# Hybrid DeltaNet, window-attention and PEER block on one core: four token blocks gathered instead of three, part of the gathering placed between mixers and retrievals

## The chip, the cores and the metric

The kernel runs on one core of a Trainium2 chip. The time is device microseconds of one execution. Three runs of the kernel before took 3164.12, 3176.35 and 3185.84 us; the median is 3176.35 us. All matrix products are split in two float parts each (a high part and a rest), so one product is three matmuls.

## The reference, cut to what matters

One decoder layer over 1024 tokens of width 1024, in 8 blocks of 128 tokens.

```python
h = rmsnorm(x);  z = h @ W_in                       # projection
o_A = gated_deltanet(...); o_B = sliding_window(...) # the two mixers
x = x + concat(o_A, o_B) @ W_out
# PEER: 16384 single-neuron experts, 8 heads, the best 16 each: 128 experts per token
qry = ht @ wq;  sc = qry . sub_keys;  top_k twice -> expert (T, 8, 16), gates = softmax
act = gelu(einsum("td,thkd->thk", xb, u_tab[eb]))
y   = einsum("thk,thkd->td", gb * act, v_tab[eb])
x = x + y
x = x + sigmoid(rmsnorm(x) @ W_g) * (p @ W_p);  out = rmsnorm(x)
```

Each token needs 128 rows of `u_tab` and 128 rows of `v_tab`. The kernel can get `y` of a block in two ways. **Gathered**: for each of the 128 expert slots, one indirect DMA fetches a row of 4 KB for each of the 128 tokens, and VectorE forms the dot product (u) or adds the weighted row (v). **Dense**: TensorE multiplies the block with all 16384 experts, 128 at a time, and the activations are multiplied with a gate matrix that is zero for all experts not chosen.

## The kernel before, in words

The work is written in program order with a tile framework, which reorders the instructions of each engine by a simulated time line, earlier program text first; on the chip each engine then runs its own list strictly in order. DMAs are issued by SP, the indirect ones by GpSimd (POOL).

- `upstream` (L317): `project` for tokens 0 to 511, the first mixers, `project` for tokens 512 to 1023, then four groups of two blocks: `mixers(gi + 1)` and `retrieve(gi)`. `mixers` calls `deltanet` and `swa` for each block. The projection frees its memory before the first retrieval.
- `retrieve`: the output projection and x, the norm, the queries, the scores, `first_topk` per head and half, then `topk` for each block (L739), which gives the 128 chosen experts and their gates.
- `topk` ends in two ways. For a gathered block (`ABLK`, blocks 5, 6, 7) it writes the experts' numbers into `eidx`. For a dense block (`BBLK`, blocks 0 to 4) it builds the gate matrix on chip: for every 4 tokens two one-hot comparisons on VectorE (`o`), four scalings on ScalarE, four matmuls (`bk_gm`) and a copy into `stage`; a `stage` tile holds `TB` = 32 tokens and is written to `gd` in HBM.
- `dense` (L857) runs over 32 groups of 4 expert tiles. A group loads its gates into `Gt` (one buffer, L879). For each expert tile `ur` and `vr` are loaded (512 KB each) and split (`uh`, `ul`, `vh`, `vl`), 2 x 24 matmuls of 320 columns make `bk_u`, ScalarE applies gelu, VectorE multiplies with `Gt` and makes `wh`, `wl`. After four tiles come the matmuls of 512 columns into `bk_yp` (two blocks, kept in PSUM to the end) and `bk_y` (the other blocks, added into `xB` each time).
- `gather_job` is a Python generator; each step is one indirect DMA `rows` and one VectorE operation (L839 for u, `acc` for v). `dense` takes 6 steps of it after each of its 128 expert tiles, 768 in all. `rows` has 4 buffers in the pool `gp` and, from the second gathered block on, 4 more in `gx`.
- `final` (L925): the gate of the layer input and the last norm, block by block.

Of the kernel before, what the change touches and what calls it, by code (L numbers as in the profile page):

```python
# [7 lines left out]
F32 = mybir.dt.float32  # L8
# [10 lines left out]
P = 128  # L19
T = 1024  # L20
NBLK = 8
D = 1024
DK = 8
NE = 128
# [1 line left out]
NEG = -3.0e38  # L26

GROUPS = [[0, 1], [2, 3], [4, 5], [6, 7]]
ABLK = [5, 6, 7]
BBLK = [0, 1, 2, 3, 4]  # L30
NA = len(ABLK)
GC = 4
TB = 32
GBUF = 4
GXBUF = 4
HELD = 2

CONSTS = ["ident", "ui", "sl", "ones", "iota", "mp"] + ["bm0"]
# [24 lines left out]
def block_kernel(ctx: ExitStack, tc, I, out, dbg=None):  # L63
# [8 lines left out]
    def tt(o, a, b, op):  # L72
        return V.tensor_tensor(o, a, b, op)  # L73
# [253 lines left out]
    def upstream():  # L327
        with early as em:
            dn = em.enter_context(tc.tile_pool(name="dn", bufs=1, reuse_waits="tile"))
            psum(em, dn=2, de=1, sw=1)  # L330
            with ExitStack() as es:
                c1 = es.enter_context(tc.tile_pool(name="c1", bufs=1, side="right"))
                wp = es.enter_context(tc.tile_pool(name="wp", bufs=3, side="right"))
                sm = es.enter_context(tc.tile_pool(name="sm", bufs=2, side="right"))
                psum(es, acc=2, tp=2)
                projected(wp, sm)
                load_consts()
                mixw = row(c1, "mix_norm", D)
                convw = c1.tile([P, 12, 4], F32, name="convw")
                nc.sync.dma_start(convw, I["convw"])  # L340
                onorm = row(c1, "out_norm", P)
                V.tensor_scalar(onorm, onorm, 0.5, None, op0=ALU.mult)
                dtb = row(c1, "dt_bias", 4)
                nea = row(c1, "a_log", 4)
                S.activation(nea, nea, AF.Exp)
                V.tensor_scalar(nea, nea, -1.0, None, op0=ALU.mult)
                prevs = c1.tile([P, 12, 3], F32, name="prevs")
                halo[:] = [(mixw, convw, onorm, dtb, nea), prevs]
                rope_tables(sm, cos, sin)
                project(0, (c1, wp, sm))  # L350
                mixers = mixing(dn)
                mixers(0)
                project(1, (c1, wp, sm))
            with ExitStack() as es:
                lt = es.enter_context(tc.tile_pool(name="lt", bufs=1, side="right", reuse_waits="tile"))
                retrieve = retrieving(lt, es)
                for gi in range(len(GROUPS)):
                    if gi + 1 < len(GROUPS):
                        mixers(gi + 1)
                    retrieve(gi)  # L360
# [20 lines left out]
    def retrieving(lt, es):  # L381
# [14 lines left out]
        def retrieve(gi):  # L396
# [9 lines left out]
            for ti in range(4):  # L406
                cs = slice(ti * 256, (ti + 1) * 256)
                pcs = [bank("s3", [256]) for _ in range(nb)]
                for dh in range(4):
                    wh, wl = weights([w[ti * 2 + dh // 2][:, 2 * (dh % 2):2 * (dh % 2) + 2] for w in woc],  # L410
                                     [P, 2, 256])
                    for bi in range(nb):
                        bs_ = slice(bi * P, (bi + 1) * P)
                        for k in range(2):
                            dk = 2 * dh + k
                            mm3(pcs[bi], mTh[:, dk, bs_], mTl[:, dk, bs_], wh[:, k], wl[:, k],
                                dk == 0, dk == DK - 1)
                for bi in range(nb):
                    tt(xts[bi][:, cs], pcs[bi], xts[bi][:, cs], ALU.add)
            h2 = hp.tile([P, 2, DK, N], F32R, tag="h2", name="h2")  # L420
            h2h, h2l = h2[:, 0], h2[:, 1]
            for bi, b in enumerate(grp):
# [13 lines left out]
            for q4 in range(4):  # L436
                qT = []
                keysT = sm.tile([P, 4, P], F32, tag="keysT", name="keysT", bufs=1)
                nc.sync.dma_start(keysT, I["keysT"][:, 4 * q4:4 * q4 + 4])
                for q in range(4 * q4, 4 * q4 + 4):  # L440
                    whs = [weights([w[q][:, 4 * dh:4 * dh + 4] for w in wqc], [P, 4, P]) for dh in range(2)]
                    pq = bank("s3", [N])
                    for dk in range(DK):
                        wh, wl = whs[dk // 4]
                        mm3(pq, wh[:, dk % 4], wl[:, dk % 4], h2h[:, dk], h2l[:, dk], dk == 0, dk == DK - 1)
                    qt = sm.tile([P, N], F32, tag="qt", name="qt", bufs=4)
                    copy(qt, pq)
                    qT.append(qt)
                for bi in range(nb):
                    pk = bank("s3", [4, P])  # L450
                    for i in range(4):
                        mm(pk[:, i], qT[i][:, bi * P:(bi + 1) * P], keysT[:, i])
                    sc = lt.tile([P, 4, P], F32, tag="sc", name="sc", bufs=2)
                    copy(sc, pk)
                    for i in range(4):
                        first_topk(lt, sc[:, i], tv[bi][:, 4 * q4 + i], tiu[bi][:, 4 * q4 + i])
            for bi, b in enumerate(grp):
                topk(lt, bg, b, tv[bi], tiu[bi])

        return retrieve  # L460

# [51 lines left out]
    def deltanet(dn, dn_state, b, qkv_d, zc_d, g, beta, eg, mTh, mTl, cols):  # L513
        def t4(tag, bufs=1):
            return dn.tile([P, 4, P], F32, tag=tag, name=tag, bufs=bufs)

        qkv = dn.tile([P, 12, P], F32, tag="qkv", name="qkv", bufs=2)
        nc.sync.dma_start(qkv, qkv_d)
        zs = t4("zs")
        nc.sync.dma_start(zs.rearrange("p a b -> p (a b)"), zc_d[:, 0:512])  # L520
# [65 lines left out]
        for l in range(1, 7):  # L586
# [20 lines left out]
            if l < 6:  # L607
                px = bank("dn", [4, P])
                for h in range(4):
                    tr(px[:, h], Y[:, h])  # L610
                X = t4("X")
                copy(X, px)
        kb = scaled("kb", 4, cf[:, 2])
        vb = scaled("vb", 8, cf[:, 3])
        qg = scaled("qg", 0, cf[:, 0])
# [37 lines left out]
    def swa(dn, state, b, zc_d, cos, sin, sink, mTh, mTl, cols):  # L653
# [70 lines left out]
        copy(mTh[:, 4:8, cols], po)  # L724
        tt(mTl[:, 4:8, cols], po, mTh[:, 4:8, cols], ALU.subtract)
        state["kv"] = (kz, vz)

    MP = C["mp"]

# [8 lines left out]
    def topk(tk, bg, b, v, iu):  # L738
# [13 lines left out]
        for h in range(8):  # L752
            c = cand[:, h]
            V.max(out=bs[:, h, 0:8], in_=c)
            V.max_index(out=pu[:, h, 0:8], in_max=bs[:, h, 0:8], in_values=c)
            V.match_replace(out=c, in_to_replace=bs[:, h, 0:8], in_values=c, imm_value=NEG)
            V.max(out=bs[:, h, 8:16], in_=c)
            V.max_index(out=pu[:, h, 8:16], in_max=bs[:, h, 8:16], in_values=c)
        pos = tk.tile([P, 16, 8], BF, tag="pos", name="pos")
        V.tensor_copy(pos.rearrange("p k h -> p h k"), pu)  # L760
        dx = tk.tile([P, 16, 8], BF, tag="dx", name="dx")
# [11 lines left out]
        for k0 in range(0, 16, KC):  # L773
# [11 lines left out]
            tt(ge, bc(st, 1, 16), bc(sel_b[:, 2], 2, KC), ALU.is_equal)  # L785
            tt(t3, ge, bc(ix[:, 1], 2, KC), ALU.mult)
            summed(i2.rearrange("p (h k) -> p k h", h=8)[:, ks], t3)

        ga = gate_a[:, ABLK.index(b)] if b in ABLK else bg.tile([P, P], F32, tag="ga", name="ga")
        gv = ga.rearrange("p (h k) -> p h k", k=16)  # L790
# [16 lines left out]
        for tb in range(P // TB):  # L807
            stage = bg.tile([P, NE, TB], F32, tag="stage", name="stage", bufs=2)
            for t8 in range(TB // NTK):
# [7 lines left out]
                for q in range(NTK // 4):  # L817
# [2 lines left out]
                        mm(pg[:, i], o2[:, 4 * q + i], o1[:, 4 * q + i])  # L820
                    t0 = t8 * NTK + 4 * q
                    copy(stage[:, :, t0:t0 + 4].rearrange("p e t -> p t e"), pg)
            nc.sync.dma_start(gd[(b - BBLK[0]) * (P // TB) + tb], stage)

    def gather_block(gp, a):
# [3 lines left out]
        dots = gp.tile([P, P], F32, tag="dots", name="dots", bufs=1)  # L829

        def rows(tab, s):
            r = (gx if a and s % 2 else gp).tile([P, D], F32, tag="rows", name="rows")
            G.indirect_dma_start(out=r, out_offset=None, in_=tab,  # L833
                                 in_offset=bass.IndirectOffsetOnAxis(ap=eidx[:, a, s:s + 1], axis=0))
            return r
# [14 lines left out]
            yield  # L850
        nc.sync.dma_start(x1d[b], acc)

    def gather_job(gp):
        for a in range(NA):
            yield from gather_block(gp, a)

    def dense(xB):  # L857
        with ExitStack() as es:
            gp = es.enter_context(tc.tile_pool(name="gp", bufs=GBUF, reuse_waits="tile"))
            pp = es.enter_context(tc.tile_pool(name="pp", bufs=1, reuse_waits="tile"))  # L860
            up = es.enter_context(tc.tile_pool(name="up", bufs=2, reuse_waits="tile"))
            ap = es.enter_context(tc.tile_pool(name="ap", bufs=2, reuse_waits="tile"))
# [9 lines left out]
            nparts = (NT + 511) // 512  # L872
            step = (NT // nparts + TB - 1) // TB * TB
            parts = [(n0, min(step, NT - n0)) for n0 in range(0, NT, step)]
            total = NA * 2 * P
            job = gather_job(gp)
            done = 0
            for cg in range(NE // GC):
                Gt = ap.tile([P, NT // TB, GC, TB], F32, tag="Gt", name="Gt", bufs=1)  # L879
                nc.sync.dma_start(Gt.rearrange("p t g k -> p t (g k)"),  # L880
                                  gd[:, :, cg * GC:(cg + 1) * GC, :].rearrange("t p g k -> p t (g k)"))
                vs, ws = [], []
                for ci in range(GC):
# [23 lines left out]
                        copy(wh[:, n0:n0 + n], ge)  # L907
                        tt(wl[:, n0:n0 + n], ge, wh[:, n0:n0 + n], ALU.subtract)
                    ws.append((wh, wl))
                    want = total * (c + 1) // NE  # L910
                    while done < want and next(job, "end") != "end":
                        done += 1
                for bi in range(NB):
                    for j in range(2):
                        cs = slice(j * 512, (j + 1) * 512)
# [6 lines left out]
                                ci == 0 and (cg == 0 or not keep), ci == GC - 1 and (cg == NE // GC - 1 or not keep))  # L922
                        if not keep or cg == NE // GC - 1:
                            tt(xB[:, bi, cs], py, xB[:, bi, cs], ALU.add)
            for _ in job:  # L925
                pass

    def final(xB):
# [52 lines left out]
                post(*cur)  # L981

    upstream()
    gx = ctx.enter_context(tc.tile_pool(name="gx", bufs=GXBUF, side="right", reuse_waits="tile"))
    with tc.tile_pool(name="xB", bufs=1, side="right", reuse_waits="tile") as xp:
        xB = xp.tile([P, NB, D], F32, name="xB")
        dense(xB)
# [60 lines left out]
```

## Time and profile before

| | |
|---|---|
| median of three runs | 3176.35 us (3164.12 to 3185.84) |
| span of the profiled execution, the only time that the profile gives for it | 3163.2 us |
| busy in that span | PE 2984.4, VectorE (DVE) 2601.3, ScalarE (ACT) 1296.5, GpSimd (POOL) 1028.0 us |
| moved by DMA | 869.38 MB, 275 GB/s on average |
| issued in `dense` | 768 gathers (402.70 MB), 128 `ur` and 128 `vr` (512 KB each), 32 `Gt` (1280 KB each) |

PE is TensorE's matmuls, PEld its weight loads. Busy times are unions: an instruction can begin some 0.1 us before the one ahead of it has ended. The DMA share is the mean busy share of the core's 16 DMA engines. The granted clock is a share of 2.4 GHz.

### The profile page before, as it was taken

Reading aid. Unit: us, or ns where it says so; the run is one execution under the profiler, and the core shown is the slowest. Engines: PE = TensorE matmul, PEld = TensorE weight load, DVE = VectorE, ACT = ScalarE, POOL = GpSimd, SP = SyncE. Lnnn points to the kernel's source line nnn. Section 1 sums busy time; section 2 is a strip of 40 time slices with the busy share of each in tenths; the row PEclk is TensorE's granted clock in tenths of the full one; section 3 lists DMA queues with packets and bytes.
Section 4 is the critical chain, followed back from the end, with each engine's and each line's share of the span. In section 5 each row is a group of like instructions: output and inputs, shape, how many; then the busy total and the mean of one; then the engine's idle time right before and its main releaser. Section 6 shows DMA issues by size and latency. Waiting matters only on the chain. (4 is left out here: it accounts for less than half of the span.)

```text
span 3163.2 us, 50802 instructions
## 1 busy us (share of the span) xinstructions
PE 2984.4 (94%) x18287; PEld 2704.4 (85%) x18287; DVE 2601.3 (82%) x6191; ACT 1296.5 (41%) x2761; POOL 1028.0 (32%) x804
## 2 busy tenths in 40 slices
PE   7989989999897889899999999999999999999998
PEld 5878989899897878778888887988899889898887
DVE  6668636999899899789888887988988878799876
ACT  5577534488887862123222222222222122222232
POOL 0000000000000014445455565555565645566600
PEclk9999999999999999999999999999999999999999
DMA  7569566667578678778889888998998888999932
GB/s 232 159 240 353 171 213 225 207 228 248 199 242 321 235 274 283 279 263 298 292 297 316 305 310 310 338 353 304 340 334 309 315 317 321 327 328 345 334 140 87
DMA packets 366188, 869.38 MB, mean 275 GB/s; under 512 B 29296, under 2 KB 153584, under 8 KB 363120
## 3 DMA queue, kind: packets, MB, share of 16 engines
q1 hardware_dynamic: 255344, 463.43, 43.1%
q0 software_dynamic: 110592, 402.70, 35.3%
q8 instruction: 144, 2.36, 0.3%
q14 instruction: 108, 0.88, 0.1%
HBM read 766.40 MB, written 99.61 MB: 274 GB/s over the span
## 5 line engine op out<-in xcount | busy, mean ns | idle before, releaser
L128 PE MATMUL bk_u<-hT,uh 128*128 128x320 f32 x4096 | 919.4, 311 | 16.1 <-ACT ge L904 16.1
L833 POOL DMA_INDIRECT rows<-in_u_dram,eidx x384 | 495.1, 1289 | 893.6 <-DVE tiu L732 469.1
L128 PEld LDWEIGHTS bk_u<-hT,uh 128*128 128x128 f32 x4096 | 698.2, 189 | 36.6 <-ACT ge L904 19.3
L833 POOL DMA_INDIRECT rows<-in_v_dram,eidx x384 | 523.5, 1363 | 401.9 <-DVE acc L76 283.5
L128 PE MATMUL bk_u<-hT,ul 128*128 128x320 f32 x2048 | 635.8, 311 | 0.2 <-DVE ul L73 0.2
L76 DVE SCALAR_TENSOR_TENSOR acc<-rows,dots,acc 128x1024 f32<-128x1024 f32 x384 | 492.0, 1281 | 44.5 <-DMA rows<-in_v_dram,eidx 41.3
L839 DVE CUSTOM_DVE_ANT_0 rows<-rows,h2n 128x1024 f32<-128x1024 f32 x384 | 461.8, 1221 | 37.3 <-DMA rows<-in_u_dram,eidx 31.5
L128 PEld LDWEIGHTS bk_u<-hT,ul 128*128 128x128 f32 x2048 | 387.5, 189 | 5.0 <-DVE ul L73 0.5
L904 ACT ACTIVATE ge<-bk_u 128x320 f32<-128x320 f32 x256 | 110.3, 432 | 642.1 <-PE bk_u L128 541.9
L128 PE MATMUL bk_y<-vh,wh 128*128 128x512 f32 x768 | 313.1, 408 | 40.2 <-DVE xB L73 38.2
L70 ACT ACTIVATE wh<-ge 128x320 fp32r<-128x320 f32 x256 | 119.0, 470 | 525.6 <-DVE ge L73 466.7
L128 PE MATMUL bk_y<-vl,wh 128*128 128x512 f32 x768 | 308.5, 402 | 0.0
L128 PE MATMUL bk_y<-vh,wl 128*128 128x512 f32 x768 | 304.3, 402 | 2.2 <-DVE wl L73 1.8
L128 PE MATMUL bk_gm<-o,o 128*128 128x128 f32 x1280 | 205.4, 292 | 29.6 <-ACT o L70 27.6
L70 ACT ACTIVATE o<-o,tT 128x128 f32<-128x128 f32 x640 | 202.4, 396 | 40.0 <-DVE o L73 34.7
L73 DVE TENSOR_TENSOR o<-iota,tT 128x512 f32<-128x512 f32 x320 | 205.4, 686 | 13.8 <-PE bk_gm L128 12.9
L128 PE MATMUL bk_yp<-vh,wh 128*128 128x512 f32 x512 | 202.3, 400 | 13.5 <-ACT wh L70 13.5
L128 PEld LDWEIGHTS bk_gm<-o,o 128*128 128x128 f32 x1280 | 182.2, 200 | 37.1 <-ACT o L70 33.9
L73 DVE TENSOR_TENSOR ge<-ge,Gt 128x320 f32<-128x320 f32 x256 | 123.7, 487 | 108.7 <-DMA Gt<-gd 95.2
L128 PEld LDWEIGHTS bk_y<-vh,wh 128*128 128x128 f32 x768 | 147.8, 192 | 76.2 <-DVE xB L73 43.2
L128 PE MATMUL bk_s<-h,whi 128*128 128x256 f32 x1024 | 206.8, 294 | 5.2 <-ACT h L70 1.5
L128 PE MATMUL bk_yp<-vl,wh 128*128 128x512 f32 x512 | 201.8, 398 | 0.0
(308 smaller groups left out, 6001.8 us busy)
## 6 DMA issues: line engine op xcount, KB each, us to landing
ur<-in_uT_dram SPq DMA_DIRECT2D x128, 512.0 KB
vr<-in_v_dram SPq DMA_DIRECT2D x128, 512.0 KB
gd<-stage SPq DMA_DIRECT2D x20, 2048.0 KB
Gt<-gd SPq DMA_DIRECT2D x32, 1280.0 KB
wlo<-wqc SPq DMA_DIRECT2D x128, 256.0 KB
whi<-wqc SPq DMA_DIRECT2D x128, 256.0 KB
whi<-woc SPq DMA_DIRECT2D x64, 256.0 KB
wlo<-woc SPq DMA_DIRECT2D x64, 256.0 KB
```

Source lines behind the costliest of these rows:

```text
L70: return S.activation(o, i, AF.Copy, **k)
L73: return V.tensor_tensor(o, a, b, op)
L76: return V.scalar_tensor_tensor(o, a, s, b, op0, op1, **k)
L128: PE.matmul(o, l, r, start=start, stop=stop)
L833: G.indirect_dma_start(out=r, out_offset=None, in_=tab, in_offset=bass.IndirectOffsetOnAxis(ap=eidx[:, a, s:s + 1], axis=0))
L839: V.tensor_tensor_reduce(out=u, in0=u, in1=h2n, op0=ALU.mult, op1=ALU.add, scale=1.0, scalar=0.0, accum_out=dots[:, s:s + 1])
L904: S.activation(ge, pa, AF.Gelu_apprx_tanh)
```

## The change

Blocks 0 to 3 are gathered and blocks 4 to 7 are dense, so there are 1024 gather steps instead of 768, and `dense` works on 512 tokens instead of 640, as one part of 512 columns instead of two of 320. The pool `gp` is opened when the projections are done. `tick(us)` stands at places in the mixers and in the retrieval; it adds `us` x `RATE` (0.55) to a credit, and for each whole credit one gather step is written there, as far as the blocks that are through `topk` allow. What is left is spread over the 128 expert tiles of `dense`. `gx` has 6 buffers, is open from the start of `dense` and serves every second step there. `TB` is 16, and `Gt` has two buffers. `qkv`, the input of `deltanet`, has one buffer instead of two.

```diff
-ABLK = [5, 6, 7]
-BBLK = [0, 1, 2, 3, 4]
+ABLK = [0, 1, 2, 3]
+BBLK = [4, 5, 6, 7]
-TB = 32
+TB = 16
-GXBUF = 4
+GXBUF = 6
+RATE = 0.55
...
                 project(1, (c1, wp, sm))
+            pools["gp"] = ctx.enter_context(tc.tile_pool(name="gp", bufs=GBUF, side="right", reuse_waits="tile"))
...
                     tt(xts[bi][:, cs], pcs[bi], xts[bi][:, cs], ALU.add)
+                    tick(0.5)
...
                         first_topk(lt, sc[:, i], tv[bi][:, 4 * q4 + i], tiu[bi][:, 4 * q4 + i])
+                        tick(1.7)
             for bi, b in enumerate(grp):
                 topk(lt, bg, b, tv[bi], tiu[bi])
+                ready[0] = sum(1 for a in ABLK if a <= b)
+                tick(2.0)
...
-        qkv = dn.tile([P, 12, P], F32, tag="qkv", name="qkv", bufs=2)
+        qkv = dn.tile([P, 12, P], F32, tag="qkv", name="qkv", bufs=1)
...   deltanet, after each of its 6 levels
+            tick(1.0)
...   end of swa
+        tick(6.0)
...   topk: after each of 8 heads, after each of 4 chunks, after each 4 tokens of gates
+            tick(1.2)
+            tick(5.0)
+                tick(1.4)
...
-            r = (gx if a and s % 2 else gp).tile([P, D], F32, tag="rows", name="rows")
+            r = (pools["gx"] if "gx" in pools and s % 2 else gp).tile([P, D], F32, tag="rows", name="rows")
...
+    pools = {}
+    ready = [0]
+    paced = {"credit": 0.0, "done": 0, "job": None}
...
+    def advance(n):
+        if paced["job"] is None:
+            paced["job"] = gather_job()
+        limit = ready[0] * 2 * P
+        while n > 0 and paced["done"] < limit and next(paced["job"], "end") != "end":
+            paced["done"] += 1
+            n -= 1
+
+    def tick(us):
+        paced["credit"] += us * RATE
+        n = int(paced["credit"])
+        paced["credit"] -= n
+        advance(n)
...
-            total = NA * 2 * P
-            job = gather_job(gp)
-            done = 0
+            first = paced["done"]
+            total = NA * 2 * P - first
             for cg in range(NE // GC):
-                Gt = ap.tile([P, NT // TB, GC, TB], F32, tag="Gt", name="Gt", bufs=1)
+                Gt = ap.tile([P, NT // TB, GC, TB], F32, tag="Gt", name="Gt", bufs=2)
...
-                    want = total * (c + 1) // NE
-                    while done < want and next(job, "end") != "end":
-                        done += 1
+                    advance(first + total * (c + 1) // NE - paced["done"])
...
-            for _ in job:
+            for _ in paced["job"]:
                 pass
```

## Rows read from the trace of the kernel before

**Rows 1.** Stages: us, busy PE, PEld, DVE, ACT, POOL (instructions), clock, DMA share, GB/s.

```profile
0.00:625.00 625.00, 578.63 (x4065) 525.35 (x4066) 420.75 (x1357) 340.16 (x828) 8.29 (x32) 0.98 0.68 226
625.00:1161.00 536.00, 481.66 (x3841) 464.55 (x3839) 505.01 (x2104) 439.15 (x1088) 1.03 (x4) 0.96 0.70 244
1161.00:3052.00 1891.00, 1826.91 (x9939) 1635.51 (x9940) 1596.11 (x2496) 476.22 (x778) 1018.64 (x768) 0.98 0.88 310
3052.00:3163.00 111.00, 97.22 (x448) 78.99 (x446) 79.46 (x239) 40.99 (x68) 0.00 (x0) 0.95 0.26 91
```

**Rows 2.** The same view, four short windows.

```profile
700.00:800.00 100.00, 99.13 (x845) 96.98 (x845) 98.73 (x420) 86.58 (x220) 0.00 (x0) 1.00 0.70 240
1000.00:1030.00 30.00, 23.07 (x146) 21.32 (x147) 25.20 (x71) 25.80 (x62) 0.00 (x0) 0.94 0.97 393
1150.00:1180.00 30.00, 18.92 (x106) 18.04 (x107) 26.15 (x111) 12.13 (x19) 8.91 (x7) 0.77 0.87 321
2200.00:2300.00 100.00, 100.00 (x558) 90.27 (x558) 90.00 (x100) 25.03 (x44) 58.25 (x45) 1.00 0.97 345
```

**Rows 3.** The tile `get` of `topk`: ns min/median/max, first to last start.

```profile
L73 DVE TENSOR_TENSOR get<-pos,sel_b x32: 405/418/428, 588.8 to 1620.0; 128x512 bf16<-128x512 bf16 x32
```

**Rows 4.** Groups of instructions: busy us, mean ns | idle before.

```profile
L128 PE MATMUL bk_gm<-o,o 128*128 128x128 f32 x1280 | 205.4, 292 | 29.6 <-ACT o L70 27.6 <-ACT stage L70 1.9
```

**Rows 5.** VectorE in order of time, in the retrievals: start, us, operation.

```profile
700.34 1.27 DVE L73 TENSOR_TENSOR o<-iota,tT 128x512 f32<-128x512 f32 x2
701.53 0.29 DVE L73 TENSOR_TENSOR get<-get 128x256 bf16<-128x256 bf16 x1
```

**Rows 6.** VectorE in order of time, in `dense`: start, us, operation.

```profile
2199.61 1.22 DVE L73 TENSOR_TENSOR vl<-vr,vh 128x1024 fp32r<-128x1024 f32 x1
2200.74 1.22 DVE L73 TENSOR_TENSOR ul<-ur,uh 128x1024 fp32r<-128x1024 f32 x1
...
2202.28 1.28 DVE L76 SCALAR_TENSOR_TENSOR acc<-rows,dots,acc 128x1024 f32<-128x1024 f32 x1
2203.48 0.49 DVE L73 TENSOR_TENSOR ge<-ge,Gt 128x320 f32<-128x320 f32 x1
...
2705.45 0.69 DVE L73 TENSOR_TENSOR xB<-bk_y,xB 128x512 f32<-128x512 f32 x1
2706.05 1.22 DVE L839 CUSTOM_DVE_ANT_0 rows<-rows,h2n 128x1024 f32<-128x1024 f32 x1
...
2707.19 1.22 DVE L839 CUSTOM_DVE_ANT_0 rows<-rows,h2n 128x1024 f32<-128x1024 f32 x1
```

**Rows 7.** Stages by tile, 1161 to 1700: `get`, then `cand`.

```profile
1161.00:1700.00 539.00, 38.07 (x136) 0.97 0.84 290
...
1161.00:1700.00 539.00, 0.00 (x0) 0.00 (x0) 20.52 (x165) 0.97 0.84 290
```

**Rows 8.** DMA queues, 1161 to 3052: packets, MB, share of 16 engines.

```profile
q0 software_dynamic: 110592, 402.70, 59.0%
q1 hardware_dynamic: 121023, 182.47, 28.7%
```

**Rows 9.** DMA queues and issues, 1890 to 1915: one `Gt`, one `ur`.

```profile
q1 hardware_dynamic: 2718, 1.83, 23.6%
...
Gt<-gd SPq DMA_DIRECT2D x1, 1280.0 KB
ur<-in_uT_dram SPq DMA_DIRECT2D x1, 512.0 KB
```

**Rows 10.** The chain that ended last, inside `dense`: start, us, what.

```profile
2372.24 14.07 PE bk_u L128 x96
...
2553.52 2.80 PE bk_y L128 x12
```

**Rows 11.** Waits over the span: us in total, times, longest.

```profile
DVE ge L73 <- DMA Gt<-gd: 95.2, 19, 8.6
...
DVE acc L76 <- DMA rows<-in_v_dram,eidx: 41.3, 36, 5.8
...
ACT junk L524 <- DMA qkv<-qkvn: 12.2, 6, 4.3
```

More of the change, by code (lines that the diff above doesn't have):

```diff
@@ L851, in gather_block, with gather_job @@
         nc.sync.dma_start(x1d[b], acc)
-    def gather_job(gp):
+    pools = {}
+    ready = [0]
+    paced = {"credit": 0.0, "done": 0, "job": None}
+    def gather_job():
         for a in range(NA):
-            yield from gather_block(gp, a)
+            yield from gather_block(pools["gp"], a)
+    def advance(n):
[10 more added lines that the diff above has]
+        advance(n)
     def dense(xB):
         with ExitStack() as es:
-            gp = es.enter_context(tc.tile_pool(name="gp", bufs=GBUF, reuse_waits="tile"))
             pp = es.enter_context(tc.tile_pool(name="pp", bufs=1, reuse_waits="tile"))
@@ L983, in block_kernel @@
     upstream()
-    gx = ctx.enter_context(tc.tile_pool(name="gx", bufs=GXBUF, side="right", reuse_waits="tile"))
+    pools["gx"] = ctx.enter_context(tc.tile_pool(name="gx", bufs=GXBUF, side="right", reuse_waits="tile"))
     with tc.tile_pool(name="xB", bufs=1, side="right", reuse_waits="tile") as xp:
```

## The prediction, made before the changed kernel ran

> **What bounds the kernel now.** I read the stage table first, then the DMA queues, then the chain of waits and single stretches of VectorE. In the stage table [rows 1] the reader sees four stages of 625, 536, 1891 and 111 us: projections with the first mixers and retrieval, later mixers and retrievals, `dense`, `final`. In the second, PE is busy 90% and VectorE 94% of the time: there is hardly an idle VectorE to fill. In `dense` PE is busy 97%, VectorE 84%, the DMA engines 88%. PE is the bound there: the chain's long pieces are `bk_u` at 14.07/96 = 0.147 us per 320 columns and `bk_y` at 2.80/12 = 0.233 us per 512 [rows 10], so one expert tile costs 48 x 0.147 + 30 x 0.233 = 14.0 us, times 128 = 1797 of the 1891 us. But the DMA engines stand close behind, at 0.97 and 345 GB/s in a window where PE has no gap [rows 2].
>
> **How many gathers move.** Nothing can be gathered before block 0's `topk` has ended; its first selection starts at 588.8 [rows 3], so I start the moved work at 625. From there the ticks in program order are 2.0 + 29.6 + 2.0 (end of group 0), 24 per pair of mixers (6 x 1 + 6 per block, two pairs left), 121.6 in group 1 (4 + 54.4 + two `topk` at 31.6) and 211.2 in groups 2 and 3 each (44.8 more per block for its gates): 625.6, times 0.55 = 344 steps, never held back by the limit of 256 per finished block. These are 216 u and 128 v steps; 680 of the 1024 (296 u, 384 v) remain for `dense`, 5.3 per expert tile instead of 6.
>
> **Stage 2, VectorE.** Costs are from start to start, since neighbours overlap: a u step 1.14 us, a v step 1.20, a split of 1024 columns 1.13, an `xB` addition 0.60 [rows 6]; a 512-column operation 1.19/2 = 0.60 [rows 5].
> - Work now 505 us [rows 1].
> - One dense block fewer: 64 one-hot comparisons x 0.60 = -38. PE loses 205.4/5 = 41 us [rows 4], which shortens nothing if VectorE sets the pace.
> - The moved steps: 216 x 1.14 + 128 x 1.20 = +400.
> - Blocks 6 and 7 are now dense, so their `topk`, which today runs beside `dense`, must be done before the first `Gt`: 38.1 + 20.5 = +59 [rows 7].
>
> That makes 926 us. VectorE's share is 0.94 there today and gathers fill some gaps, so I take 0.96: 965 us. Bounds: 0.99, as in its fullest 100 us (935), and 0.88, as between 1150 and 1180 (1052) [rows 2].
>
> Beside it lie the transfers: 0.70 x 536 = 375 us of all 16 engines, plus 344 gathers at 0.59 x 1891/768 = 1.453 us [rows 1, 8] = 500, minus 24 for a block's gates (8.4 MB at 351 GB/s, which is 310/0.88), so 851 of 965. POOL needs 1018.64/768 = 1.33 us per gather [rows 1], 456 us; a wait of POOL for a free `rows` buffer now has the mixers' small POOL operations (`kz`, `vz`) queued behind it, and `swa` waits for them. I cost that, the 4 buffers and the single `qkv` buffer at nothing, because VectorE has other blocks' work to do. If that cover is gone, `qkv` costs at most a load of 0.79 MB per block, 3.5 us at 226 GB/s, 28 us in all; today its wait is 12.2 us [rows 11].
>
> **Dense, three limits.**
> - PE: 24 matmuls of 512 columns for u and 24 for y, 48 x 0.233 = 11.2 us, times 128 = 1434 us, so 363 less.
> - VectorE: per expert tile two splits 2.26, two 512-column operations 1.20, one `xB` addition (two blocks instead of three) 0.60, together 4.06, times 128 = 520; the gathers 296 x 1.14 + 384 x 1.20 = 798. Sum 1318 us.
> - DMA engines, in us of all 16: gathers 680 x 1.453 = 988; `ur` and `vr`, 256 transfers of the same size, 372. For `Gt`, the hardware queue took 23.6% of 25 us = 5.90 us for one `Gt` and one `ur` [rows 9], so a `Gt` costs 4.45 us now, 27.8 ns per packet of 512 B on one engine; a 4 KB packet takes 1.453 x 16/128 = 182 ns. Sixteen tokens make packets of 256 B, 4096 per load instead of 2560. A straight line through the two sizes gives 16.8 ns, 4.31 us a load, 138 in all; cost by bytes alone gives 114, the 512 B price per packet 228. I take 138, which is nearest to how the two known sizes behave. The rest of the stage's transfers: 0.287 x 1891 - 372 - 32 x 4.45 = 29. Sum 1527, with bounds 1503 and 1617.
>
> So the DMA engines, not PE, become the bound of `dense`. The best 100 us reached 0.97 [rows 2]; with ten row buffers instead of eight I take 0.98: 1558 us. What could be cheaper: those 0.97 windows hold packets that may run faster; the 30 us at 393 GB/s [rows 2] say so, and then PE's 1434 at 0.99 = 1448 is the floor. What could be dearer: 1617/0.95 = 1702.
>
> **The second Gt buffer** takes away VectorE's 95.2 us of waiting [rows 11] and frees the weight loads queued behind that issue on SP. I count it as zero: late next are the row transfers themselves.
>
> **Sum.** 625 + 965 + 1558 + 111 = 3259 us against the profiled span of 3163. `final` reads one block more from HBM and is left at 111. The profile gives no time for its execution but the span; the median of the runs is 13 above that, which I add: 3272 us. Stage 2 grows by 429, `dense` shrinks by 333.
>
> **Rivals.**
> 1. *Faster: `dense` stays bound by PE.* It moves 356 + 134 + 34 = 524 MB, so this needs 362 GB/s held for 1448 us. For it: 393 GB/s at 0.97 in one window. Against: 345 at 0.97 with gathers running [rows 2]. With VectorE at 0.99 in stage 2: 625 + 935 + 1448 + 111 + 13 = 3132.
> 2. *No change.* Stage 2 at 0.98 (945) and `dense` at the full-share rate of 352 GB/s, 1490: 3184. For it: 0.99 and 0.97 stand in single windows [rows 2]; against: both must hold for a thousand microseconds.
> 3. *Stage 2 gets worse than its work.* The gather steps stand in VectorE's strict order, so a row that lands late holds up `topk` and the mixers behind it. PE has 441 us of work in 965, and where it had gaps its granted clock fell: 0.77 with 18.92 of 30 us busy [rows 2]. Against: in `dense` v rows cost VectorE only 41.3 us of waiting [rows 11]. With 0.88: 1052 and 3359.
> 4. *Small packets cost as much as those of 512 B.* 1617/0.98 = 1650, and 3364. No row here has a load in runs of 256 B. The Trainium skill, DMA: Bandwidth & Descriptors, section Specifications, speaks for this rival: it puts the smallest transfer for line rate at 512 B and says that below it the engine reads, modifies and writes; by it the sum is this rival's, by the straight line the forecast's. The rows here show only that 512 B already runs at 18 instead of 22.5 B/ns.
> 5. *The change does not do what it says:* the reordering finds no room on VectorE and leaves all 1024 steps to `dense`. Stage 2 is then 526/0.96 = 548 and `dense` (1024 x 1.453 + 372 + 29 + 138)/0.98 = 2068: 3365.
>
> **How the numbers follow.** Forecast 0.42, rival 1 0.12, rival 2 0.18, rival 3 0.15, rival 4 0.10, rival 5 0.03. The runs of before spread by 0.7%, so about 1% can be told from no change: faster means under 3145, slower over 3208. Faster 0.12; same 0.18; slower the other four, 0.70. The range is 3150 to 3410: it holds rivals 2 to 5 and leaves out most of rival 1 and the corner where 0.88 and 1702 come together (3503). Without rivals 1 and 2, the slower cases alone lie between 3210 and 3410.
>
> **What would show it.** In the profile after: some 340 gathers before `dense`, whose first `ge` comes near 1590; VectorE at 0.95 or more from 625 on; `dense` about 1560 long with PE clearly below 97% and a DMA share of 0.95 to 0.98; few waits for `Gt`. The prediction is wrong if PE is still without gaps in `dense`, if the DMA engines move over 360 GB/s there, or if stage 2 ends before 1500.

## The result, and the profile after

The changed kernel takes 3414.07 us (median of four runs, 3407.39 to 3421.47); the kernel before, on the same chip, 3172.83 us. The ratio is 1.0745, with a 95% interval of 1.0708 to 1.0783: slower, as forecast, but by 241 us and not by 96, and 4 us above the upper end of the range. The profiled execution has a span of 3419.7 us.

The page of the changed kernel: the span, each engine's busy time, PE's busy share and granted clock in 40 slices of 85 us, and the DMA queues (packets, MB, share of 16 engines).

```profile
span 3419.7 us, 42638 instructions
...
PE 2758.4 (81%) x14188; PEld 2333.4 (68%) x14188; DVE 2782.6 (81%) x6193; ACT 1173.3 (34%) x2343; POOL 1359.9 (40%) x1060
...
PE   7999989886765862151579988899999889999988
...
PEclk9999999997787965555589999999999999999999
...
q0 software_dynamic: 147456, 536.94, 44.2%
...
q1 hardware_dynamic: 304736, 446.65, 38.8%
```

PE worked 226 us less than before and VectorE 181 us more. The hole in PE's row, slices 16 to 20, is the end of the second stage. The stages of the kernel after, with the columns of [rows 1]; the last row is the second part of the second stage.

```profile
0.00:625.00 625.00, 580.66 (x4018) 526.80 (x4018) 409.88 (x1289) 329.49 (x788) 7.05 (x30) 0.97 0.66 220
625.00:1735.00 1110.00, 618.03 (x3626) 562.24 (x3626) 1001.74 (x3117) 398.90 (x975) 503.74 (x415) 0.70 0.87 305
1735.00:3305.00 1570.00, 1463.19 (x6096) 1164.41 (x6096) 1289.42 (x1530) 402.58 (x513) 849.07 (x615) 0.97 0.92 317
3305.00:3420.00 115.00, 96.53 (x448) 79.98 (x448) 81.61 (x259) 42.30 (x70) 0.00 (x0) 0.92 0.30 105
1240.00:1735.00 495.00, 172.26 (x717) 149.04 (x716) 421.90 (x888) 199.79 (x453) 284.10 (x222) 0.55 0.82 284
```

Against [rows 1] the second stage grew from 536 to 1110 us (+574) and `dense` shrank from 1891 to 1570 (-321). The forecast was +429 and -333: the second stage is where it failed. The same view for the tile `rows` alone (columns: VectorE, POOL, clock, DMA share, GB/s) counts the gather steps.

```profile
625.00:1735.00 1110.00, 493.13 (x399) 502.27 (x409) 0.70 0.87 305
1735.00:3305.00 1570.00, 777.09 (x625) 849.07 (x615) 0.97 0.92 317
1240.00:1735.00 495.00, 266.26 (x215) 284.10 (x222) 0.55 0.82 284
```

399 steps ran before `dense`, not 344. By the prediction's count the ticks wrote 344 there; the other 55 the framework's reordering pulled ahead from the text of `dense`. VectorE in order of time shows what the last 495 us look like (start, us, operation, idle before it and what ended that).

```profile
1354.25 1.28 DVE L77 SCALAR_TENSOR_TENSOR acc<-rows,dots,acc 128x1024 f32<-128x1024 f32 x1 [0.29 <-DMA rows<-in_v_dram,eidx]
1355.45 0.42 DVE L74 TENSOR_TENSOR get<-get,dx 128x512 bf16<-128x512 bf16 x1
1356.35 1.28 DVE L77 SCALAR_TENSOR_TENSOR acc<-rows,dots,acc 128x1024 f32<-128x1024 f32 x1 [0.47 <-DMA rows<-in_v_dram,eidx]
1357.55 0.28 DVE L74 TENSOR_TENSOR get<-get 128x256 bf16<-128x256 bf16 x1
```

The short operations of `topk`, 0.3 to 0.4 us each, alternate with gather steps of 1.28 us that wait for their rows. The waits between 1240 and 1735 say who stands behind them (us in total, times, longest).

```profile
PE bk_gm L132 <- DVE cand L74: 181.6, 4, 98.9
...
PEld bk_gm L129 <- ACT o L71: 151.0, 80, 5.4
PE bk_gm L129 <- ACT o L71: 129.1, 78, 5.1
...
DVE rows L850 <- DMA rows<-in_u_dram,eidx: 38.7, 29, 4.1
```

PE is idle until `topk` has made `cand`, and then goes at the pace of the scalings of `o`. VectorE's own waiting for rows is small beside its 422 us of work, though it ends most of the 73 us in which VectorE is idle there.

In `dense` the gathers end before PE does. The stage, cut where the last gather is issued:

```profile
1735.00:3190.00 1455.00, 1352.01 (x5624) 1074.74 (x5625) 1233.48 (x1462) 371.75 (x473) 847.61 (x615) 0.97 0.96 332
3190.00:3305.00 115.00, 111.18 (x474) 89.68 (x472) 55.94 (x69) 30.83 (x40) 1.47 (x1) 0.99 0.40 127
```

While gathers run the DMA share is 0.96, against 0.88 over [rows 1]'s `dense`. Then there are none left, and for 115 us PE works by itself at a share of 0.40. The queues and issues of the first 1455 us:

```profile
q0 software_dynamic: 88859, 323.55, 61.1%
q1 hardware_dynamic: 162160, 158.82, 34.3%
...
Gt<-gd SPq DMA_DIRECT2D x30, 1024.0 KB, 18.3
```

### The profile page after: what moved, and what is told of

The parts are those of the page before. It is cut to its first block, busy times and chain, and to the rows that moved or that the text cites. A ratio compares the mean times of both kernels' runs of the same rounds, so it can differ in the third digit from the quotient of the medians.

```text
span 3419.7 us, 42638 instructions
## 1 busy us (share of the span) xinstructions
PE 2758.4 (81%) x14188; PEld 2333.4 (68%) x14188; DVE 2782.6 (81%) x6193; ACT 1173.3 (34%) x2343; POOL 1359.9 (40%) x1060
## 4 chain that ended last, share of the span: by engine, by line
PE 41%; DVE 20%; issue 14%; DMA 13%; POOL 8%; ACT 4%; SPq 0%; POOLq 0%; DVEq 0%; ACTq 0%
PE bk_u L129 10%; POOL rows L844 8%; PE bk_acc L129 7%; DVE rows L850 5%; PE bk_y L129 5%; PE bk_yp L129 5%; DMA rows<-in_u_dram,eidx 5%; PE bk_s L129 4%; PE bk_g L129 3%; PE bk_dn L129 2%; DVE o L74 2%; DVE acc L77 2%; DMA ur<-in_uT_dram 2%; DMA rows<-in_v_dram,eidx 2%; PE bk_gm L129 1%
## 5 line engine op out<-in xcount | busy, mean ns | idle before, releaser
L844 POOL DMA_INDIRECT rows<-in_v_dram,eidx x512 | 695.2, 1358 | 588.9 <-DVE acc L77 356.0
L844 POOL DMA_INDIRECT rows<-in_u_dram,eidx x512 | 656.2, 1282 | 609.0 <-DVE dots L850 299.6
L77 DVE SCALAR_TENSOR_TENSOR acc<-rows,dots,acc 128x1024 f32<-128x1024 f32 x512 | 656.7, 1283 | 33.2 <-DMA rows<-in_v_dram,eidx 22.3
L129 PE MATMUL bk_u<-hT,uh 128*128 128x512 f32 x2048 | 643.5, 395 | 30.1 <-ACT uh L71 19.7
L129 PEld LDWEIGHTS bk_u<-hT,uh 128*128 128x128 f32 x2048 | 388.1, 190 | 119.9 <-ACT uh L71 25.3
L129 PE MATMUL bk_u<-hT,ul 128*128 128x512 f32 x1024 | 403.3, 394 | 8.1 <-DVE ul L74 7.8
L129 PE MATMUL bk_yp<-vh,wh 128*128 128x512 f32 x512 | 206.7, 421 | 59.9 <-ACT wh L71 59.7
L129 PEld LDWEIGHTS bk_u<-hT,ul 128*128 128x128 f32 x1024 | 194.1, 190 | 54.6 <-DVE ul L74 12.5
L129 PEld LDWEIGHTS bk_s<-h,whi 128*128 128x128 f32 x1024 | 172.2, 206 | 37.2 <-ACT sc L71 10.3
L74 DVE TENSOR_TENSOR vl<-vr,vh 128x1024 fp32r<-128x1024 f32 x128 | 156.3, 1221 | 34.1 <-ACT vh L71 34.0
L74 DVE TENSOR_TENSOR ul<-ur,uh 128x1024 fp32r<-128x1024 f32 x128 | 156.2, 1221 | 31.0 <-ACT uh L71 30.8
```

The lines of the kernel that those rows point to most:

```text
L77: return V.scalar_tensor_tensor(o, a, s, b, op0, op1, **k)
L129: PE.matmul(o, l, r, start=start, stop=stop)
L844: G.indirect_dma_start(out=r, out_offset=None, in_=tab, in_offset=bass.IndirectOffsetOnAxis(ap=eidx[:, a, s:s + 1], axis=0))
```

## The experiments

All kernels are edits of the kernel after, but for e3, e4, e8, e12 and e13, which are edits of the one before; stage rows have the columns of [rows 1]. The two theories at the start. **A, place:** gather steps stand ahead of the last blocks' `topk` and gates in VectorE's strict order; move them out of there and most of the loss goes. **B, sum of work:** a step costs about its VectorE time wherever it is put before `dense`, `dense` can take no more of them, and place matters little. Times are medians; ratios are to the kernel before, with 95% intervals.

### e1_no_tail_ticks, e2_rate0: fewer ticks

```diff
-                tick(2.0)           # and the ticks of 1.2, 5.0 and 1.4 in topk
+                if b < 6:
+                    tick(2.0)
```


> The changed kernel without the gather ticks in topk and in the gate building of blocks 6 and 7 (84 of the 344 steps by program order). Theory A: the stage before dense is long because, after the last retrieval, gather steps stand ahead of the gate building in VectorE's strict order and wait for rows, while TensorE idles. Then the stretch from 1240 to the first dense gelu, 495 us in the changed kernel, falls to 200-300, dense grows by 120-200, total 3290-3350. Theory B: the stage is bound by VectorE's sum of work, so moving 84 steps moves about 100 us from one stage to the next: total 3380-3450.

3361.17 us, 1.0605 [1.0558, 1.0652]. The second stage of e1, then its gather steps (the view for `rows`):

```profile
625.00:1692.00 1067.00, 619.88 (x3626) 563.09 (x3626) 980.20 (x3095) 399.62 (x976) 479.84 (x395) 0.70 0.88 308
...
625.00:1692.00 1067.00, 467.68 (x379) 478.15 (x389) 0.70 0.88 308
```

```diff
-RATE = 0.55
+RATE = 0.0
```


> The changed kernel with RATE 0: all 1024 gather steps are written into dense, 8 per expert tile. Theory A (the steps placed upstream cost more there than they save): first dense gelu at 1200-1300, dense bound by the DMA engines at (1024 x 1.453 + 372 + 29 + 138)/0.96 = 2110, total 3420-3520. Theory B (the placement upstream is worth its gathers): dense also about 2110, but first gelu no earlier than 1350 since the gates of blocks 6 and 7 need their time anyway: 3570 or more.

3359.27 us, 1.0573 [1.0542, 1.0605]. The second stage of e2, its `dense` and what follows, then the gather steps of the second stage:

```profile
625.00:1375.00 750.00, 554.73 (x3628) 511.43 (x3626) 687.54 (x2715) 389.75 (x976) 152.97 (x137) 0.82 0.72 256
1375.00:2915.00 1540.00, 1456.11 (x6094) 1159.56 (x6095) 1312.53 (x1553) 400.74 (x512) 907.06 (x647) 0.98 0.96 334
...
2915.00:3356.00 441.00, 110.85 (x452) 88.63 (x450) 390.68 (x650) 44.28 (x73) 279.60 (x246) 0.63 0.86 324
...
625.00:1375.00 750.00, 146.19 (x122) 150.77 (x131) 0.82 0.72 256
```

With no tick at all 122 steps still ran before `dense`, and in e1 379: the reordering fills in. So neither took the gathers out, both times lie outside what either theory had said, and these two do not decide between A and B: the stage had to be emptied by a dependency. What they do show is the ticks' own cost, 3414 - 3359 = 55 us, under a quarter of the loss.

### e5_no_gather_before_gates, e6_pause_in_tail: gathers held back

```diff
+            if b == BBLK[-1] and tb == P // TB - 1:
+                ef = eidx.rearrange("p a s -> p (a s)")
+                stt(ef, stage.rearrange("p e t -> p (e t)")[:, 0:NA * P], 0.0, ef, ALU.mult, ALU.add)
+                held_back[0] = NA * 2 * P
...
+    held_back = [0]                 # e6: [185]
-        limit = ready[0] * 2 * P
+        limit = min(ready[0] * 2 * P, held_back[0])
```

The experts' numbers are written again, unchanged, once the last gates are there, so that no later gather can start earlier.

> The changed kernel in which the experts' numbers are rewritten (unchanged) by an operation that reads the last gate tile, so that no gather can start before the gates are done; all 1024 steps follow. In the run with RATE 0 the reordering still put about 100 gathers ahead of dense and the first dense gelu came at 1375. Theory A (gather steps in VectorE's strict order stretch the gate building at the end): first gelu at 1180-1280. Theory B (four late dense blocks have a long gate building by themselves): first gelu at 1350 or later. Dense and the gathers behind it then take (1024 x 1.453 + 539)/0.96 = 2110, total 3400-3500.

3455.32 us, 1.0883 [1.0856, 1.091]. Stages of e5, then the gather steps of the last one:

```profile
625.00:1271.00 646.00, 511.88 (x3614) 481.07 (x3612) 556.66 (x2454) 379.19 (x962) 5.47 (x9) 0.89 0.55 193
1271.00:2853.00 1582.00, 1463.83 (x6096) 1163.91 (x6096) 1325.90 (x1695) 400.83 (x513) 954.24 (x672) 0.97 0.94 331
2853.00:3448.00 595.00, 112.43 (x448) 89.70 (x448) 518.07 (x751) 43.63 (x71) 395.63 (x349) 0.59 0.89 335
...
2853.00:3448.00 595.00, 448.30 (x357) 395.63 (x349) 0.59 0.89 335
```

> The changed kernel with its ticks, but after 185 gathers (as many as it had done by 1240) none until the last gate tile is built. Theory A: the first dense gelu comes at 1400-1450 instead of 1735, dense has 839 gathers to carry, (839 x 1.453 + 539)/0.96 = 1831, total 3350-3400. Theory B: the stretch after 1240 stays above 350 us, first gelu after 1600, total over 3500.

3370.43 us, 1.0616 [1.0589, 1.0643]. Stages of e6, and its stretch from 1240 on:

```profile
625.00:1463.00 838.00, 575.62 (x3604) 525.69 (x3603) 754.40 (x2761) 382.29 (x964) 220.16 (x194) 0.81 0.73 264
1240.00:1463.00 223.00, 134.79 (x714) 118.85 (x712) 176.70 (x545) 184.01 (x448) 4.17 (x5) 0.81 0.27 113
1463.00:3045.00 1582.00, 1461.85 (x6096) 1160.36 (x6096) 1342.28 (x1670) 400.12 (x510) 957.02 (x682) 0.97 0.95 334
3045.00:3364.00 319.00, 109.31 (x448) 86.62 (x448) 276.49 (x461) 43.87 (x73) 176.96 (x154) 0.66 0.81 305
```

A is right on the tail: without gathers the stretch from 1240 to `dense` takes 223 us and not 495. It is wrong on what that is worth: the steps come later, behind `dense`, and the whole gains 44 us; with all of them behind the gates (e5) it loses 41. Three prices follow.
- Before `dense`, a step costs (1735 - 1271)/399 = 1.16 us in the kernel after, (1692 - 1271)/379 = 1.11 in e1, (1463 - 1271)/185 = 1.04 in e6, (1375 - 1271)/122 = 0.85 in e2: near its VectorE time of 1.14 to 1.20 [rows 6], so that at most a quarter of it is filled in for nothing.
- Behind `dense`, e5's last stage is 595 us against 115 for `final` alone: 480/357 = 1.34 us a step.
- Within `dense` a step more does not show: the stage takes 1570 us with 625 steps, 1548 with 645 (e1), 1540 with 647 (e2), 1582 with 668 (e5) and with 678 (e6). How many stand there was settled when the framework laid out VectorE's list, not on the chip; but with a DMA share of 0.92 to 0.96 there is room for some 65 more at most, an estimate from 0.98 at 1.453 us each.

### e7_last_four_gathered, e14_blocks_0_1_6_7: which blocks are gathered

```diff
-ABLK = [0, 1, 2, 3]
-BBLK = [4, 5, 6, 7]
+ABLK = [4, 5, 6, 7]        # e14: [0, 1, 6, 7]
+BBLK = [0, 1, 2, 3]        # e14: [2, 3, 4, 5]
-RATE = 0.55
+RATE = 0.0
```


> The changed kernel with blocks 4 to 7 gathered and 0 to 3 dense, RATE 0: as many gathers, the gates early as in the kernel before. Theory A (late gates are what costs, not the fourth gathered block): first dense gelu at 1100-1170, then 1024 gathers bound by the DMA engines, 2110 us at 0.96: total 3370-3420. If the fourth block alone made the loss, the stage before dense would still be short and the total the same as the changed kernel's 3414 or above.

3315.97 us, 1.0446 [1.042, 1.0473]. Stages of e7, then the gather steps of the last one:

```profile
625.00:1076.00 451.00, 412.53 (x3269) 396.10 (x3267) 428.33 (x1803) 364.94 (x925) 8.27 (x10) 0.96 0.69 244
1076.00:2668.00 1592.00, 1485.23 (x6406) 1194.52 (x6406) 1386.74 (x2257) 417.36 (x537) 881.42 (x635) 0.98 0.93 326
2668.00:3312.00 644.00, 108.02 (x448) 86.48 (x448) 564.23 (x796) 44.01 (x72) 425.22 (x384) 0.58 0.89 336
...
2668.00:3312.00 644.00, 492.74 (x393) 425.22 (x384) 0.58 0.89 336
```

> The changed kernel with blocks 0, 1, 6, 7 gathered, 2 to 5 dense, RATE 0. With blocks 4 to 7 gathered it took 3316, with 0 to 3 and RATE 0 3359. If late dense blocks are the harm: no long gate building at the end, gathers start near 650, total 3200-3280. If early gathering itself is the harm: 3320-3370.

3374.12 us, 1.0635 [1.0603, 1.0668]. The second stage of e14:

```profile
625.00:1270.00 645.00, 515.03 (x3621) 483.41 (x3619) 586.83 (x2436) 382.99 (x962) 72.83 (x75) 0.88 0.70 248
```

With the four blocks at the end, as before, `dense` starts at 1076; 393 steps are left behind it, (644 - 115)/393 = 1.35 us each. This is the fastest kernel with four gathered blocks, and it is 4.5% slower than the one before. Against it the first four blocks and their ticks lose about 100 us more. The larger part, 4.5%, comes with the fourth block at the end; e7 also has the other buffers and `TB` = 16, and these were not run apart. e14 is not the way out: its dense blocks 4 and 5 still hold up `dense` until 1270, with 64 steps done by then, and it is slower than e7 and no faster than e2. Neither time was foreseen: e7 is 54 us under its first case, e14 4 us over its second.

### e3_before_first3, e13_halves_blocks_0_6_7: early blocks in the kernel before

```diff
-ABLK = [5, 6, 7]
-BBLK = [0, 1, 2, 3, 4]
+ABLK = [0, 1, 2]           # e13, on e4 below: [0, 6, 7]
+BBLK = [3, 4, 5, 6, 7]     # e13: [1, 2, 3, 4, 5]
```


> The kernel before with blocks 0, 1, 2 gathered instead of 5, 6, 7, nothing else changed: all 768 steps in dense. Theory A: dense blocks at the end must have their topk and gates done before the first dense gelu, with TensorE idle beside them; first gelu 1161 -> 1280-1330, total 3290-3340. Theory B: only the topk work of two blocks (59 us) moves ahead, and dense loses it: total within 1.5% of 3173.

3517.0 us, 1.108 [1.1059, 1.1101]. Two windows of e3:

```profile
1200.00:1300.00 100.00, 13.04 (x51) 11.09 (x51) 78.40 (x180) 13.36 (x30) 56.62 (x46) 0.50 0.78 262
3100.00:3200.00 100.00, 100.00 (x549) 89.55 (x548) 35.18 (x50) 24.92 (x40) 0.00 (x0) 1.00 0.31 95
```

> The kernel before with Gt in halves and blocks 0, 6, 7 gathered, 1 to 5 dense. If late dense blocks are the harm: first dense gelu at 1170-1260 as block 5's gates come late in the third group, block 0's rows are partly done by then, the gathers no longer end after dense, total 3090-3140. If early gathering itself is the harm (VectorE has no room before dense): first gelu at 1300 or later, total 3180-3260.

3271.75 us, 1.0311 [1.0282, 1.034]; the first gelu of `dense` starts at 1346, against 1166 in e4, though only 70 gathers ran before 1240.

No ticks and three gathered blocks, and in e3 still the same picture: PE at 13% in the middle, and `dense` alone at the end with the DMA engines at 0.31. Both theories had e3 far too fast, and it changes two things at once, early gathers and late dense blocks. e13 comes nearer to parting them, since its last dense block is in the same group of two as that of e4, though one later: `dense` starts 179 us later, and the 110 steps done by then are 128 us at the price of 1.16. By that estimate early gathering does harm without ticks and without a fourth block too.

### e4_before_gt_halves, e8_halves_and_pace, e12_halves_more_buffers: the Gt wait alone

```diff
-                Gt = ap.tile([P, NT // TB, GC, TB], F32, tag="Gt", name="Gt", bufs=1)
...
+                    if ci % 2 == 0:
+                        Gt = ap.tile([P, NT // TB, 2, TB], F32, tag="Gt", name="Gt", bufs=2)
+                        nc.sync.dma_start(Gt.rearrange("p t g k -> p t (g k)"),
+                                          gd[:, :, c:c + 2, :].rearrange("t p g k -> p t (g k)"))
```


> The kernel before with Gt loaded for two expert tiles at a time into two buffers of half the size (same memory, runs of 256 B instead of 512 B). If the wait for Gt (95 us of VectorE, TensorE idle 64 us in dense) is what one buffer costs: 3110-3150. If the row transfers are what is late next, or the smaller runs cost twice as much: 3160-3210.

3151.59 us, 0.9925 [0.989, 0.9961].

```diff
-                    want = total * (c + 1) // NE
+                    want = min(total, total * (c + 1) * 10 // (NE * 9))
```


> The kernel before with Gt in halves, and with the gather steps paced a ninth faster through dense. With halves alone TensorE ended dense some 65 us earlier, but the gathers ended 85 us after it. If program order decides when they run: they end with dense, total 3100-3135. If the row buffers or the DMA engines decide: 3140-3165.

3148.58 us, 0.9909 [0.9882, 0.9935].

```diff
-            r = (gx if a and s % 2 else gp).tile([P, D], F32, tag="rows", name="rows")
+            r = (gx if s % 2 else gp).tile([P, D], F32, tag="rows", name="rows")
```


> The kernel before with Gt in halves, the faster pace, and both row pools used from the first gathered block on (8 row buffers instead of 4 for block 5). If four row buffers hold back the first third of the gathers: the gathers end 40-80 us earlier than 3068, total 3090-3125. If the DMA engines or VectorE do: 3140-3160.

3166.81 us, 0.9953 [0.9938, 0.9967]. Two half-size gate tiles in the room of the one take the wait for `Gt` away, and that is worth 24 us of the 95 in [rows 11]. The stretch of [rows 1]'s `dense` in e4:

```profile
1166.00:3052.00 1886.00, 1831.18 (x10064) 1642.74 (x10064) 1604.54 (x2547) 495.58 (x802) 977.77 (x761) 0.99 0.90 308
```

The last `ge` comes at 2965 instead of 3027, but the gathers now end later than PE. The other pace (e8) adds nothing that can be told from e4, and more row buffers (e12) take part of the gain back. e8 has the lowest time of all, 0.9% under the kernel before, and is not told apart from e4.

### e9_six_row_buffers, e15_two_weight_buffers, e11_two_qkv_buffers: the buffers

```diff
-GBUF = 4
+GBUF = 6                    # in e9 alone; the rest in e9 and e15
-GXBUF = 6
+GXBUF = 4
-        wp = es.enter_context(tc.tile_pool(name="wp2", bufs=4, side="right", reuse_waits="tile"))
+        wp = es.enter_context(tc.tile_pool(name="wp2", bufs=2, side="right", reuse_waits="tile"))
```


> The changed kernel with 6 instead of 4 row buffers in gp (and 4 instead of 6 in gx, so dense has ten as before; the weight buffers of the retrieval go from 4 to 2 to make room). Theory A1 (in the stretch after 1240 four row buffers limit how fast the gather steps that stand in VectorE's way are worked off): VectorE's share there rises from 0.85 to 0.92 or more and the total falls by 20-60 us, to 3355-3395. Theory A2 (the DMA engines limit it, at 0.82 with four rows in flight): within 15 us of 3414. If two weight buffers are what is late next: over 3430.

3474.74 us, 1.0937 [1.0908, 1.0965].

> The changed kernel with two instead of four weight buffers in the retrieval and gx at 4 instead of 6: the control of the run with six row buffers (3475). If the row buffers made that run slower: within 20 us of 3414. If the weight buffers did: 3460 or more.

3436.39 us, 1.0825 [1.0801, 1.085].

```diff
-        qkv = dn.tile([P, 12, P], F32, tag="qkv", name="qkv", bufs=1)
+        qkv = dn.tile([P, 12, P], F32, tag="qkv", name="qkv", bufs=2)   # and wp2 with 3
```


> The changed kernel with two qkv buffers again (three weight buffers in the retrieval instead of four make the room). The prediction put the single buffer at nothing: within 15 us of 3414. If the single buffer delays the mixers: 28 us or more faster.

3432.7 us, 1.08 [1.0784, 1.0817]. Gather steps of e9 up to 1240:

```profile
625.00:1240.00 615.00, 318.22 (x256) 314.46 (x262) 0.72 0.91 333
```

More row buffers made it worse: up to 1240 there are 256 steps, against 217 in e15 and 184 in the kernel after, and the gate matmuls begin at 1286, against 1211 and 1097. Of e9's 61 us over the kernel after, 22 belong to the weight and `gx` buffers (e15), the rest to the two row buffers. A second `qkv` buffer, with one weight buffer less for it, makes the time 19 us longer, and the waits for `qkv` are 14.5 us with one and 17.6 with two: that the single one costs anything does not show, but the two buffers were not changed apart.

### e10_busy_tensor_engine: the clock

```diff
+                    pd = bank("dn", [4, P])
+                    for i in range(6):
+                        mm(pd[:, i % 4], ident, iota)
```

Six unused matmuls after each four gate matmuls.

> The changed kernel with six unused 128-column matmuls behind every four gate matmuls, so that TensorE is busier while the gates are built. Theory C (the low granted clock, 0.52 to 0.55 from 1300 to 1700, is what stretches the gate building): the clock there rises above 0.8 and the first dense gelu comes 80-150 us earlier, total 3270-3340. Theory A (VectorE's order and the rows set the pace): first gelu within 30 us of 1735 or later, total 3390-3480.

3411.83 us, 1.0738 [1.0715, 1.0761]. Two stretches of e10:

```profile
1085.00:1240.00 155.00, 151.78 (x1322) 151.14 (x1322) 145.55 (x423) 85.54 (x193) 56.98 (x43) 0.99 0.92 329
1300.00:1700.00 400.00, 119.24 (x495) 104.30 (x494) 339.50 (x788) 135.77 (x309) 214.53 (x180) 0.53 0.81 280
```

The reordering put the extra matmuls early. There the granted clock rose from 0.86 to 0.99 and nothing came of it; from 1300 to 1700 it stayed at 0.53 in both. So this run says nothing on theory C, and what the low clock costs in the tail stays open.

## Why the prediction was right or wrong

**The bound, and dense.** 1558 forecast, 1570 measured, and that this is so near is partly luck. The DMA engines' work was sized well: with the 625 steps that were really left, the same terms make 625 x 1.453 + 372 + 29 + 138 = 1447 us of all 16 engines; measured are 0.96 x 1455 + 0.40 x 115 = 1443. The share was not: 0.98 throughout was assumed, and 0.92 came out, since the gathers ran out 115 us early. By the forecast's own rule 625 steps would have taken 1447/0.98 = 1477 us; 55 steps fewer and a lower share cancelled each other. PE was busy for 1463 us where 1434 were forecast, 93% of the stage. That the DMA engines are the bound is not shown: VectorE waits only 9.6 us for u rows there, and PE's longest wait, 59.7 us, is for ScalarE's `wh`. Two limits lay close together.

**Small packets.** Of q1's 0.343 x 1455 = 499 us, 235 `ur` and `vr` are 341 at the prediction's 1.453 and the small transfers some 25 by its 29 for the whole stage; what is left over 30 `Gt` loads is about 4.4 us each, an estimate, where the straight line gave 4.31, bytes alone 3.6 and rival 4's price 7.1. Rival 4 is out: 256 B cost some 17 ns a packet by this estimate, and 512 B 27.8. The rule of the Trainium skill, DMA: Bandwidth & Descriptors, section Specifications, that below 512 B the engine reads, modifies and writes, shows no such cost in these loads.

**The second Gt buffer.** The wait fell from 95.2 to 4.4 us. Counting it as zero fits this kernel, which was not run with one buffer; in the kernel before, e4 shows the wait worth 24 us.

**Stage 2: the step that failed**, "926 us. VectorE's share is 0.94 there today and gathers fill some gaps, so I take 0.96: 965 us". Measured 1110, so 145 of the 161 us by which the span exceeds the forecast's 3259 (`dense` 12, `final` 4); the median lies 6 under the span and not 13 over it. Two parts:
- *VectorE's work*, 1002 us and not 926: 79 us at 0.96. e5 measures the stage without gathers at 557, where I had 505 - 38 + 59 = 526; the 59 counted two tiles of `topk`, `get` and `cand`, and left out others, such as `tkr` with 7.5 us in the same window. The gathers then take 1002 - 557 = 445 us for 399 steps, where I had 400 us for 344; each was cheaper than I had it (1.12 against 1.16), but the reordering, left out of the count, added 55 steps.
- *VectorE's share*, 0.90 and not 0.96: the other 66 us. VectorE is idle for 108 us in the kernel after, 87 in e1, 84 in e6, 62 in e2, and 89 in e5 with no gather there; but 31 in [rows 1] and 23 in e7. What e5 has and e7 has not is that the last retrieved blocks are dense, so `topk`, one-hot, scaling, matmul and copy of the last gates stand at the end with no later mixers or retrievals beside them. In e5 the last gate matmul comes 238 us after the last matmul of the queries, in e14 113, in the kernel before 6, in e7 84 ahead of it; the idle time falls in the same order, 89, 58, 31, 23. I had costed the buffers at nothing "because VectorE has other blocks' work to do", and did not ask where that work ends.

The waits of VectorE in that stage, first in the kernel after (two), then in e5:

```profile
DVE rows L850 <- DMA rows<-in_u_dram,eidx: 50.3, 42, 4.1
DVE acc L77 <- DMA rows<-in_v_dram,eidx: 22.3, 29, 2.2
...
DVE o L74 <- PE bk_gm L129: 42.9, 52, 2.2
```

With gathers there, 73 of the 108 us end with a late row; without them VectorE waits instead for the gate matmuls to free `o`. That the rows do not make the gap is shown by e5, and by e9 beside e15: waits for rows fall from 59 to 22 us, and VectorE's idle time is 112 us against 111. How much of the 66 us each wait makes is not parted further.

**The rivals.** Rival 1 is out: 317 GB/s in `dense`, not 362. Rival 2 needed stage 2 in 945 us. Rival 3 came nearest in the share, 0.88, and the late rows of its reason are there, 73 us of them; but the gap is nearly as long without gathers, and with its 926 us of work it still ends 55 us short, at 3359. Rival 5: 399 steps ran early, so it is out; e5, which forces its first half, takes 646 us there and not 548.

**Where the expected gain went.** `dense` gave 321 us. The second stage took 574: 110 from 536 to e5's 646, which is the stage without gathers, and the other 464 for 399 steps, which is what the price of 1.16 is worked out from; with 4 in `final` that is the 257 us between the spans. The steps cost so much because `dense` holds some 625 to 680 of them in its 1540 to 1592 us, where the longer one of before held all 768, and there are now 1024: some 345 to 400 have no cover, at 0.85 to 1.35 us each, before or behind `dense`. In versions, each with all that stands ahead of it: the fourth gathered block at the end and the new buffers, +4.5% (e7); the first four blocks instead, +5.7% (e2); the ticks, +7.4%.

**Left open:** what the clock of 0.52 to 0.55 costs in the tail (the gate matmuls are busy for 225 us in the kernel after and for 165 in e7, whose second stage has 0.96, so up to some 60 us of PE's time hang on it, an estimate, and not yet time of the stage), and how the kernel would run if the reordering left the steps where the text has them; that wasn't tried.

## What to carry to other kernels

Before work is moved into a stage, look at how the stage ends: a chain that has lost its neighbours leaves gaps that no average share of the stage shows. When a long stage is shortened, count again what it was hiding; here 321 us of `dense` went together with the room for over 100 gathers. And a reordering framework fills in what pacing leaves out, so count the steps in the trace, not in the text.

## What the runs showed of the hardware

Packets of 256, 512 and 4096 B cost about 17, 27.8 and 182 ns on one DMA engine, nearly a straight line; all three are estimates from the queues' shares, the first two with `ur` taken at the price of a gather. With gathers running, the DMA engines held a share of 0.96 at 332 GB/s over 1455 us, and 326 to 334 GB/s in `dense` of e2, e5, e6 and e7; the 393 GB/s of a 30 us window without gathers [rows 2] was not reached over any of these. PE's granted clock was 0.55, close to the lower of its two levels (0.5, which is 1.2 GHz), over 495 us in which PE was 35% busy, and 0.97 in `dense`, where it was busy 93%.
